# Layer 0: output projection of seven token tiles as partial sums in SBUF beside the last pair of heads; compressed keys' sections by token halves

## The chip, the cores and the metric

The kernel runs on one core of a Trainium2 chip. The metric is the device time of one execution in microseconds (us); the kernel before was timed in three runs.

## What is computed

A decoder trunk of two layers over 1024 tokens of width 1024, in float32. Layer 0 mixes with forgetting attention (FoX), layer 1 with native sparse attention (NSA); each adds its projected, gated mixer output to x, and a last RMSNorm follows.

```python
def fox_mixer(h, w_in, b_f, w_out):
    proj = h @ w_in
    q, k, v, f, z = split(proj)                      # 16 heads of 64
    c = cumsum(log_sigmoid(f + b_f))
    logits = q @ k.T * HEAD_DIM ** -0.5 + c[query] - c[key]     # causal
    o = softmax(logits) @ v
    return (o * silu(z)) @ w_out

def reference(x, ...):
    x = x + fox_mixer(rmsnorm(x, norm_g[0]), ...)
    x = x + nsa_mixer(rmsnorm(x, norm_g[1]), ...)
    return rmsnorm(x, final_g)
```

The change concerns the last product of `fox_mixer`, the sum with x behind it, and the first sections of the input projection of `nsa_mixer` (`kc_raw`, the keys to be compressed).

## The kernel before

**Products.** A float32 product is made of two-part operands (a high part rounded by a cast, a low part as the rest). `mm3` (L132) issues three matmuls per 128-row chunk: high by high, high by low, low by high. A projection of one 128-wide section for one half of the tokens (512 columns, one bank of PSUM) is eight chunks, 24 matmuls.

**Layer 0, attention.** Heads go in eight pairs. For each pair `fox_fill` projects k, v, q and z; `FoxDuo` handles two query tiles of 128 (one of each token half) of one head: score matmuls into the three score banks of `ps_s` (L587, L588), a running minimum on VectorE, DVE (L596, into `P`), exp on ScalarE, ACT (L605), the high part as a copy on ACT (L606) and the low part on DVE (L607), a transposing transfer on the DMA queue SP (`pT<-hl`, L608), and two duos later the PV matmuls (L621, L622) into a bank of `ps_a`, with the evictions L633 and L635. When a pair is done, `o` is transposed on PE (`pto`, L643), scaled and gated (L645) and stored to `oF` in DRAM (L646), one row block of 128 per pair and token half.

**What sets the order.** `merge` draws PE work from two generators: `fox_main` (scores and PV, with costs) and `fox_fill`. For each unit of cost of the main work it draws 2.3 units of fill (`PACE`; `LAST`, 2.6, for the last eight duos). A fill that yields a condition is blocked until it holds. On each engine the instructions stand in the order a scheduler gives them, and are executed in that order.

**Layer 0, output projection.** `load_wout` fetches half of the output weights (512 rows) into a tile, and splits them: casts on ACT, low parts (`wo<-wo,wo`, L539) on GpSimd (POOL). `out_start` runs in the fill of the last pair: for token tiles 4, 5 and 6 it loads row blocks of `oF` (`of<-oF`, L482, one staging tile `wst`), splits them (L476 on ACT, L477 on DVE) and multiplies them by the weights into PSUM banks that are kept until the end: chunks 0 to 3 of tiles 4 and 5, later 4 to 6, then 0 to 6 of tile 6, and at the end chunk 7 of all three. `out_layer` does the rest behind the attention: for tile 7 and 0 to 3 it loads all eight row blocks (L701), splits them (L702, L703) and multiplies; for each tile it adds x (`xr`, L710), squares with a sum on ACT (L94), takes the root and its inverse (L101, L102), multiplies by the inverse and the gains (`h_n`, L106), stores x (L725), and transposes h on PE (`pth_n`, L116) into `hT`, high part on ACT (L120), low part on DVE (L121).

**Layer 1, first sections.** `cmp_raw` projects a section of the compressed keys or values for both token halves; the two sections of a kind follow each other (`pn_kc`). Their weights are loaded by `load_w` (cast on DVE, L128; low part on POOL, L129) into two pairs of buffers. Behind them come the gates (`pg`, L993, L994).

## Time and profile before

| what | us |
|---|---|
| median of 3 runs (lowest to highest) | 1500.1 (1499.29 to 1501.46) |
| profiled execution, its own time | 1503.75 |
| its span, first to last instruction | 1502.0 |
| PE busy | 1418.6 (94%) |
| DVE busy | 1069.9 (71%) |
| ACT busy | 806.4 (54%) |
| POOL busy | 572.6 (38%) |

One execution was recorded; its own time lies 3.65 us above the median of the runs. The page gives busy time by engine, the same in 40 slices of 37.6 us with the clock that TensorE was granted, and the groups of instructions. Busy time of PE is modelled to the end of each pipelined matmul, so the distance between starts says what one costs.

### The profile page before, as it was taken

Reading aid. Unit: us, or ns where it says so; the run is one execution under the profiler, and the core shown is the slowest. Engines: PE = TensorE matmul, PEld = TensorE weight load, DVE = VectorE, ACT = ScalarE, POOL = GpSimd, SP = SyncE. Lnnn points to the kernel's source line nnn. Section 1 sums busy time; section 2 is a strip of 40 time slices with the busy share of each in tenths; the row PEclk is TensorE's granted clock in tenths of the full one; section 3 lists DMA queues with packets and bytes.
Section 4 is the critical chain, followed back from the end, with each engine's and each line's share of the span. In section 5 each row is a group of like instructions: output and inputs, shape, how many; then the busy total and the mean of one; then the engine's idle time right before and its main releaser. Section 6 shows DMA issues by size and latency. Waiting matters only on the chain.

```text
span 1502.0 us, 29578 instructions
## 1 busy us (share of the span) xinstructions
PE 1418.6 (94%) x10488; PEld 1176.0 (78%) x10488; DVE 1069.9 (71%) x2764; ACT 806.4 (54%) x2029; POOL 572.6 (38%) x612
## 2 busy tenths in 40 slices
PE   5999999999999877899999998989999999989998
PEld 4888888888788666788888876878888888877886
DVE  6586888787787774555745568778888888877745
ACT  5364646555565752324222465457767676766623
POOL 1232232222232610023324233356767666766500
PEclk9999999999999888999999998999999999999999
DMA  7886777877778864541524667585877796787544
GB/s 245 256 177 140 163 154 160 178 148 169 153 163 157 213 116 144 178 152 57 158 83 135 195 158 192 169 218 130 158 188 154 167 174 151 172 201 161 92 138 153
DMA packets 405875, 242.92 MB, mean 162 GB/s; under 512 B 332576, under 2 KB 353312, under 8 KB 405472
## 3 DMA queue, kind: packets, MB, share of 16 engines
q1 hardware_dynamic: 405728, 241.03, 66.5%
q8 instruction: 83, 1.36, 0.4%
q14 instruction: 64, 0.52, 0.1%
HBM read 121.16 MB, written 44.11 MB: 110 GB/s over the span
## 4 chain that ended last, share of the span: by engine, by line
PE 67%; DVE 16%; ACT 6%; DMA 5%; issue 4%; POOL 2%; SPq 0%; DVEq 0%; ACTq 0%; POOLq 0%
PE S_n L1331 6%; PE y L133 4%; PE y L135 4%; PE y L134 3%; PE ptp_n L1363 3%; PE v L133 2%; PE v L135 2%; PE v L134 2%; PE S L587 2%; PE S L588 2%; PE k L133 2%; PE O L621 2%; PE k L134 2%; DVE hl L607 2%; PE k L135 2%
## 5 line engine op out<-in xcount | busy, mean ns | idle before, releaser
L1341 ACT ACTIVATE P_n<-P_n,m_n 128x640 f32<-128x640 f32 (+7 forms) x256 | 187.4, 733 | 69.1 <-DVE m_n L1340 43.4
L1331 PE MATMUL S_n<-nk,nq 128*128 128x320 f32 (+5 forms) x768 | 178.6, 347 | 10.8 <-DVE m_n L1338 7.5
L605 ACT ACTIVATE P<-P,m 128x512 f32<-128x512 f32 (+1 forms) x192 | 116.9, 610 | 132.0 <-DVE m L596 131.2
L576 POOL TENSOR_TENSOR Bd<-B,tri 128x128 f32<-128x128 f32 x128 | 62.3, 502 | 245.4 <-DVE m L596 227.3
L1345 POOL TENSOR_TENSOR hl_n<-P_n,hl_n 128x640 f16<-128x640 f32 (+4 forms) x128 | 142.9, 1116 | 9.4
L1331 PEld LDWEIGHTS S_n<-nk,nq 128*128 128x128 f32 x768 | 126.0, 192 | 23.5 <-DVE m_n L1338 9.7
L607 DVE SCALAR_TENSOR_TENSOR hl<-P,hl 128x512 f16<-128x512 f32 (+1 forms) x192 | 124.0, 663 | 19.9 <-ACT hl L606 18.9
L1338 DVE CUSTOM_DVE_ANT_0 P_n<-S_n,wmask 128x640 f32<-128x640 f32 (+2 forms) x192 | 112.9, 595 | 23.7 <-PE S_n L1331 20.0
L1344 POOL CAST hl_n<-P_n 128x640 f16<-128x640 f32 (+4 forms) x128 | 74.8, 584 | 119.5 <-ACT P_n L1341 108.6
L150 ACT ACTIVATE pth_n<-ptp_n 128x512 f16<-128x512 f32 (+1 forms) x160 | 86.6, 546 | 54.9 <-PE ptp_n L1363 53.9
L151 DVE SCALAR_TENSOR_TENSOR ptl_n<-ptp_n,pth_n 128x512 f16<-128x512 f32 (+1 forms) x160 | 100.5, 633 | 17.0 <-ACT pth_n L150 15.4
L133 PE MATMUL y<-wo,ohi 128*128 128x512 f32 x230 | 95.4, 415 | 4.5 <-ACT ohi L702 4.5
L1363 PE MATMUL ptp_n<-ident,P_n 128*128 128x128 f32 x576 | 91.5, 279 | 5.3 <-DVE ptl_n L151 3.4
L606 ACT ACTIVATE hl<-P 128x512 f16<-128x512 f32 (+1 forms) x192 | 92.5, 513 | 4.2 <-DMA pT<-hl 2.8
L135 PE MATMUL y<-wo,olo 128*128 128x512 f32 x230 | 92.6, 404 | 1.0 <-DVE olo L703 1.0
L134 PE MATMUL y<-wo,ohi 128*128 128x512 f32 x230 | 92.8, 404 | 0.0
L1363 PEld LDWEIGHTS ptp_n<-ident,P_n 128*128 128x128 f32 x576 | 66.7, 142 | 18.8 <-DVE ptl_n L151 11.3
L587 PE MATMUL S<-KH,Q 128*128 128x512 f32 (+1 forms) x192 | 68.3, 369 | 10.0 <-DVE m L596 9.8
L1338 DVE CUSTOM_DVE_ANT_0 P_n<-S_n,bias 128x640 f32<-128x640 f32 (+1 forms) x64 | 65.1, 1018 | 9.9 <-PE S_n L1331 9.9
L1371 PE MATMUL O_n<-nv,pth_n 128*128 128x64 f16 x576 | 70.5, 195 | 1.1 <-ACT pth_n L150 0.6
L1372 PE MATMUL O_n<-nv,pth_n 128*128 128x64 f16 x576 | 69.6, 193 | 0.0
L1373 PE MATMUL O_n<-nv,ptl_n 128*128 128x64 f16 x576 | 68.4, 193 | 0.0
(398 smaller groups left out, 4530.3 us busy)
## 6 DMA issues: line engine op xcount, KB each, us to landing
nq<-qD SPq DMA_DIRECT2D x64, 256.0 KB
B<-cD SPq DMA_DIRECT2D x16, 512.0 KB
wo<-wD SPq DMA_DIRECT2D x16, 512.0 KB
nq<-qD SPq DMA_DIRECT2D x64, 128.0 KB
x<-in_x_dram SPq DMA_DIRECT2D x8, 512.0 KB
wst_k<-in_fox_w_dram SPq DMA_DIRECT2D x8, 512.0 KB
wst_v<-in_fox_w_dram SPq DMA_DIRECT2D x8, 512.0 KB
wD<-in_fox_w_out_dram SPq DMA_DIRECT2D x8, 512.0 KB
```

The source lines that it names most:

```text
L133: T.matmul(ps, wh, mh, start=first, stop=False, **kw)
L134: T.matmul(ps, wh, ml, start=False, stop=False, **kw)
L135: T.matmul(ps, wl, mh, start=False, stop=last, **kw)
L151: V.scalar_tensor_tensor(lo[:, 0:n], pt[:, 0:n], scale, h, OP.mult, OP.subtract)
L587: T.matmul(ps[:, 0:n], q, KH[j][:, k0:k0 + n], start=True, stop=False)
L605: A.activation(L[:, 0:n], L[:, 0:n], AF.Exp, bias=init, scale=-1.0, accum_out=self.lr[:, col + c:col + c + 1])
L607: V.scalar_tensor_tensor(lo[:, cs], L[:, 0:n], UP, hi[:, cs], OP.mult, OP.subtract)
L1331: T.matmul(ps[:, b, 0:w], self.q[x][:, qi * P:(qi + 1) * P], k[:, k0 + b * w:k0 + b * w + w], start=(x == 0), stop=(x == 1))
L1338: V.tensor_tensor_reduce(dst, src, mk, 1.0, 3e38, OP.add, OP.min, m)
L1341: A.activation(L, L, AF.Exp, bias=m, scale=-1.0, accum_out=self.l[:, y, qi:qi + 1])
L1345: G.tensor_tensor(hl[:, n:2 * n], L, hl[:, 0:n], OP.subtract)
L1363: T.transpose(pt[:, (x + i) * P:(x + i + 1) * P], L[:, kb * P - k0:(kb + 1) * P - k0], ident)
```

## The change

Four parts:

- `out_start` becomes `out_start0`. It works in eleven parts (token tile, first chunk, end): chunks 0 to 3 of tiles 4 to 7, chunks 4 to 6 of the same tiles, chunks 0 to 6 of tiles 0, 1 and 2. Each half of a part is one product in a bank of `ps_a`, which DVE adds at once to `xr`, a tile in SBUF that starts as x. The load and the split of a part are issued between the two halves of the part before. `out_rest0`, in place of `out_layer`, has only chunk 7 of these seven tiles and all of tile 3, then the norms.
- The tiles `KH` and `KL` move to a pool `sk` of their own that lives to the end of the layer; as the keys of a pair are used up, `xr` takes their places.
- In the last pair the order of the fill becomes q and z of tokens 512 to 1023, the first weights' load, q of 0 to 511, the weights' splits, z of 0 to 511, then `out_start0`. `load_wout` yields for each half chunk, and gives every second low part to DVE. `LAST` is gone; `merge` gets a cap of 4000 on the fill's debt.
- `cmp_raw` takes lists of sections: both sections of the compressed keys are projected for tokens 512 to 1023 first, then both for 0 to 511. The values' sections stay as they are.

```diff
+    sk = tc.alloc_tile_pool(name="sk", bufs=4, side="right")
...
-        KH = [sa.tile([P, S], F32R, tag="KH", bufs=4, name=f"KH_{p}_{j}") for j in range(2)]
+        KH = [sk.tile([P, S], F32R, tag="KH", name=f"KH_{p}_{j}") for j in range(2)]
...
-                for half in (1, 0):
-                    yield from fox_q(p, wq, (half,))
-                    yield from fox_z(p, wz, (half,))
-                    yield from load_wout(hp, 0, half)
-        yield from out_start()
+                yield from fox_q(p, wq, (1,))
+                yield from fox_z(p, wz, (1,))
+                rows0 = load_wout(hp, 0, 1)
+                yield next(rows0)
+                yield from fox_q(p, wq, (0,))
+                yield from rows0
+                yield from fox_z(p, wz, (0,))
+                yield from out_start0(load_wout(hp, 0, 0))
...
+    def out_start0(rows1):
+        yield next(rows1)
+        parts = [(t, 0, 4) for t in (4, 5, 6, 7)] + [(t, 4, 7) for t in (4, 5, 6, 7)] + [(t, 0, 7) for t in (0, 1, 2)]
+        def met(n):
+            t, _, stop = parts[n]
+            return (("o", stop - 1, t // 4) in ready and ("scored", 6) in ready
+                    and (t >= 4 or "scores" in ready))
+        def load(n):
+            t, k, stop = parts[n]
+            if t not in xs0:
+                xs0[t] = sk.tile([P, D], F32, tag=("KH", "KL")[t % 2], name=f"xr0_{t}")
+                dma(xs0[t], a["x"][t * P:(t + 1) * P, :])
+            pend[n] = wp.tile([P, KC, P], F32, tag="wst", bufs=1, name=f"of0_{t}_{k}"), *out_parts(f"0_{t}_{k}")
+            dma(pend[n][0][:, k:stop, :], oF[k * P:stop * P, t * P:(t + 1) * P].rearrange("(k p) t -> p k t", p=P))
...
+        for n, (t, k0, stop) in enumerate(parts):
+            if n == 2:
+                yield from rows1
+            more = n + 1 < len(parts)
+            soon = more and met(n + 1)
+            for half in range(2):
+                if soon:
+                    (load, split)[half](n + 1)
+                _, oh, ol = pend[n]
+                pt = ps_a(f"y0_{t}_{k0}_{half}")
+                cs = slice(half * 512, half * 512 + 512)
+                for k in range(k0, stop):
                     wh, wl = ready["wout"][k // 4]
+                    mm3(pt, oh[:, k, :], ol[:, k, :], wh[:, k % 4, cs], wl[:, k % 4, cs], k == k0, k == stop - 1)
                     yield 650
+                V.tensor_tensor(xs0[t][:, cs], pt, xs0[t][:, cs], OP.add)
+            if more and not soon:
+                yield lambda n=n: met(n + 1)
+                load(n + 1)
+                yield 1000
+                split(n + 1)
...
-        if i:
-            yield 0
+        yield 0
         for k in range(4):
             for c in range(2):
-                if i:
-                    yield 400
+                yield 400 if i else 200
...
-                (V if i and c else G).tensor_tensor(lo[:, k, cs], f(lo[:, k, cs]), f(hi[:, k, cs]), OP.subtract)
-            yield 200
+                (V if c else G).tensor_tensor(lo[:, k, cs], f(lo[:, k, cs]), f(hi[:, k, cs]), OP.subtract)
...
-    merge(fox_main(), fox_fill(), PACE, rebase=True)
+    merge(fox_main(), fox_fill(), PACE, rebase=True, cap=4000)
...
+    def out_rest0(ow, w, after):
...
+        for t in (4, 5, 6, 7, 3, 0, 1, 2):
...
+            for half, cs in enumerate(cols2):
+                pt = (ps_s, ps_a)[t % 2](f"y0_{t}_{half}")
+                if t == 3:
+                    for k in range(7):
+                        wh, wl = w[k // 4]
+                        mm3(pt, oh[:, k, :], ol[:, k, :], wh[:, k % 4, cs], wl[:, k % 4, cs], k == 0, False)
+                wh, wl = w[1]
+                mm3(pt, lh[:, tk], ll[:, tk], wh[:, 3, cs], wl[:, 3, cs], t != 3, True)
+                V.tensor_tensor(xs0[t][:, cs], pt, xs0[t][:, cs], OP.add)
+                nm.square(cs)
+            pend.append((t, xs0[t], nm.finish(gB, 2)))
+            if len(pend) > 2:
+                after(*pend.pop(0))
...
+        for part in parts:
+            yield from section([(kind, i) for i in part], lambda half, pt, n, part=part: use(half, pt, part[n]))
+        ready[kind, "raw"] = True
...
-        for i in range(2):
-            yield from cmp_raw("kc", i)
+        yield from cmp_raw("kc", ((0, 1),))
```

How instructions move is shown at three places (names with a last number that only tells buffers apart).

DVE in the last pair, around the third duo of its first head, whose scores fill `P_0_3` and whose minimum is L596 before and L604 after. Before:

```order
L596 ISA P_0_3_0_1_6479,m_0_3_0_6477<-S_0_3_0_1_6478,Bd_0_3_0_6475,m_0_3_0_6477 128x128
L596 ISA m_0_3_0_6477 128x1
L631 RECIPROCAL l_0_1_6275<-l_0_1_6275 128x2
L630 TENSOR_TENSOR l_0_2_6400<-l_0_2_6400 128x1
L596 ISA P_0_3_0_0_6485,m_0_3_0_6477<-S_0_3_0_0_6484,B_0_6176,m_0_3_0_6477 128x512
L596 ISA m_0_3_0_6477 128x1
L607 SCALAR_TENSOR_TENSOR hl_0_2_6398<-P_0_2_0_1_6418,hl_0_2_6398 128x384
L477 TENSOR_TENSOR olo_6124<-of_4_6341,ohi_6123 128x384
L607 SCALAR_TENSOR_TENSOR hl_0_2_6398<-P_0_2_0_0_6424,hl_0_2_6398 128x512
L633 TENSOR_REDUCE ot_0_1_6517<-O_0_1_6496 128x128
```

The same place after the change:

```order
L604 ISA P_0_3_0_1_6529,m_0_3_0_6527<-S_0_3_0_1_6528,Bd_0_3_0_6525,m_0_3_0_6527 128x128
L604 ISA m_0_3_0_6527 128x1
L615 SCALAR_TENSOR_TENSOR hl_0_3_6510<-P_0_3_1_0_6517,hl_0_3_6510 128x128
L604 ISA P_0_3_0_0_6535,m_0_3_0_6527<-S_0_3_0_0_6534,B_0_6161,m_0_3_0_6527 128x512
L604 ISA m_0_3_0_6527 128x1
L519 TENSOR_TENSOR xr_4_6129<-y_4_4_0_6497,xr_4_6129 128x512
L519 TENSOR_TENSOR xr_4_6129<-y_4_4_1_6552,xr_4_6129 128x512
L638 TENSOR_TENSOR l_0_3_6512<-l_0_3_6512 128x1
L639 RECIPROCAL l_0_3_6512<-l_0_3_6512 128x2
L615 SCALAR_TENSOR_TENSOR hl_0_3_6510<-P_0_3_0_1_6529,hl_0_3_6510 128x512
L615 SCALAR_TENSOR_TENSOR hl_0_3_6510<-P_0_3_0_0_6535,hl_0_3_6510 128x512
L641 TENSOR_REDUCE ot_0_1_6598<-O_0_1_6562 128x128
```

Two additions of product banks (L519) stand between a duo's minimum and its low parts; there are 22 of them in the pair.

ACT at the pair's seventh duo (`P_1_2`, `hl_1_2`). Before:

```order
L605 ACTIVATE P_1_2_1_0_6650,l_1_2_6645<-P_1_2_1_0_6650,m_1_2_1_6648 128x256
L606 ACTIVATE hl_1_2_6643<-P_1_2_1_0_6650 128x256
L605 ACTIVATE P_1_2_0_1_6663,l_1_2_6645<-P_1_2_0_1_6663,m_1_2_0_6661 128x384
L605 ACTIVATE P_1_2_0_0_6669,l_1_2_6645<-P_1_2_0_0_6669,m_1_2_0_6661 128x512
L606 ACTIVATE hl_1_2_6643<-P_1_2_0_1_6663 128x384
L606 ACTIVATE hl_1_2_6643<-P_1_2_0_0_6669 128x512
```

And after the change:

```order
L613 ACTIVATE P_1_2_1_0_6791,l_1_2_6786<-P_1_2_1_0_6791,m_1_2_1_6789 128x256
L497 CAST ohi_1_0_6915<-of_1_0_6914 128x896
L614 ACTIVATE hl_1_2_6784<-P_1_2_1_0_6791 128x256
L613 ACTIVATE P_1_2_0_1_6804,l_1_2_6786<-P_1_2_0_1_6804,m_1_2_0_6802 128x384
L613 ACTIVATE P_1_2_0_0_6810,l_1_2_6786<-P_1_2_0_0_6810,m_1_2_0_6802 128x512
L614 ACTIVATE hl_1_2_6784<-P_1_2_0_1_6804 128x384
L614 ACTIVATE hl_1_2_6784<-P_1_2_0_0_6810 128x512
```

The cast of the loaded chunks of token tile 1 (L497) stands between the first exp of the duo and its copy.

DVE in the output layer after the change, where tile 7's norm ends and tile 3's product comes in; `whi_nkc` is the weight cast for the second section of the compressed keys:

```order
L106 SCALAR_TENSOR_TENSOR h_n_7_7234<-xr_7_6353,st_n_7_7233,gB_7145 128x512 x2
L121 TENSOR_TENSOR hT_1_1_7141<-pth_n_5_1_7260,hT_1_0_7140 128x4x128
L718 TENSOR_TENSOR xr_3_7151<-y_3_0_7271,xr_3_7151 128x512
L128 CAST whi_nkc_7534<-wst_nkc_7532 128x1024
L718 TENSOR_TENSOR xr_3_7151<-y_3_1_7298,xr_3_7151 128x512
L121 TENSOR_TENSOR hT_1_1_7141<-pth_n_6_0_7331,hT_1_0_7140 128x4x128
L100 TENSOR_TENSOR st_n_3_7269<-st_n_3_7269 128x1
```

Before, the same cast stood between the two additions of tile 3 too, but tile 3 was the last of the layer; now tiles 0, 1 and 2 come behind it.

## Rows read from the trace of the kernel before

**Rows 1.** The page: the span in 40 slices, PE's busy tenths and its clock.
```profile
PE   5999999999999877899999998989999999989998
PEclk9999999999999888999999998999999999999999
```

**Rows 2.** Windows: length, PE, PEld, DVE, ACT, POOL busy; clock, DMA share, GB/s.
```profile
405.00:468.00 63.00, 63.00 (x405) 52.04 (x403) 50.90 (x152) 36.54 (x93) 17.48 (x20) 1.00 0.78 165
500.00:591.00 91.00, 72.33 (x439) 56.07 (x437) 57.31 (x183) 43.85 (x112) 25.37 (x29) 0.83 0.59 127
591.00:669.00 78.00, 70.45 (x321) 57.03 (x322) 41.65 (x74) 27.73 (x63) 8.02 (x8) 0.96 0.51 172
...
440.00:450.00 10.00, 10.00 (x61) 8.24 (x60) 9.79 (x29) 4.80 (x12) 4.17 (x5) 1.00 0.68 163
```

**Rows 3.** PE's waits, 500 to 591 (three) and 591 to 669: total, times, longest.
```profile
PE S L587 <- DVE m L596: 9.8, 9, 2.7
PE O L621 <- DMA pT<-hl: 3.1, 2, 1.9
PE O L621 <- DVE ot L633: 2.9, 2, 2.5
...
PE y L133 <- ACT ohi L702: 4.5, 2, 2.3
```

**Rows 4.** Timeline of PE at the marks: start, length, instruction.
```profile
405.08 0.38 PE L643 MATMUL pto<-ident,o 128*128 128x128 f32 x2
...
468.35 0.49 PE L643 MATMUL pto<-ident,o 128*128 128x128 f32 x3
...
507.36 0.63 PE L133 MATMUL y<-wo,ohi 128*128 128x512 f32 x1
...
590.14 0.27 PE L643 MATMUL pto<-ident,o 128*128 128x128 f32 x1
...
668.33 0.40 PE L135 MATMUL pn_kc<-hT,wlo_nkc 128*128 128x512 f32 x1
...
677.22 0.39 PE L135 MATMUL pn_kc<-hT,wlo_nkc 128*128 128x512 f32 x1
...
686.97 0.39 PE L993 MATMUL pg<-hT,gw 128*128 128x512 f32 x1
```

**Rows 5.** PE's groups, one of three alike: 500 to 591 (two), 591 to 669.
```profile
L133 PE MATMUL y<-wo,ohi 128*128 128x512 f32 x32 | 14.6, 457 | 0.0
...
L133 PE MATMUL y<-wo,o_KH 128*128 128x512 f32 x16 | 7.2, 451 | 0.0
...
L133 PE MATMUL y<-wo,ohi 128*128 128x512 f32 x80 | 32.8, 411 | 4.5 <-ACT ohi L702 4.5
...
L116 PE MATMUL pth_n<-ident,h_n 128*128 128x128 f32 x64 | 8.9, 275 | 2.6 <-DVE hT L121 1.4 <-DVE h_n L106 1.2
```

**Rows 6.** DVE's groups, 591 to 669 us: busy, mean ns, idle before and why.
```profile
L106 DVE SCALAR_TENSOR_TENSOR h_n<-xr,st_n,gB 128x512 f32<-128x512 f32 x16 | 11.5, 765 | 0.1
L710 DVE TENSOR_TENSOR xr<-y,xr 128x512 f32<-128x512 f32 x16 | 10.7, 689 | 20.1 <-PE y L135 16.1 <-DMA xr<-in_x_dram 4.0
L121 DVE TENSOR_TENSOR hT<-pth_n,hT 128x512 fp32r<-128x512 f32 x16 | 10.5, 682 | 0.2 <-ACT hT L120 0.2
L703 DVE TENSOR_TENSOR olo<-of,ohi 128x1024 fp32r<-128x1024 f32 x5 | 6.1, 1224 | 5.7 <-ACT ohi L702 5.7
```

**Rows 7.** Timeline of ACT and DVE: a cast behind a load, behind a matmul.
```profile
591.52 1.04 ACT L702 CAST ohi<-of 128x1024 fp32r<-128x1024 f32 x1 [5.26 <-DMA of<-oF]
...
661.91 0.69 DVE L128 CAST whi_nkc<-wst_nkc 128x1024 fp32r<-128x1024 f32 x1 [4.52 <-PE y L134]
```

**Rows 8.** POOL's group, 440 to 700 us; timeline of DVE, two splits.
```profile
L539 POOL TENSOR_TENSOR wo<-wo,wo 128x512 fp32r<-128x512 f32 x16 | 22.2, 1410 | 9.4 <-ACT wo L538 9.4
...
500.86 1.70 DVE L477 TENSOR_TENSOR olo<-of,ohi 128x512 fp32r<-128x512 f32 x1
...
509.76 0.68 DVE L477 TENSOR_TENSOR olo<-of,ohi 128x512 fp32r<-128x512 f32 x1
```

More of the change, by code (lines that the diff above doesn't have):

```diff
@@ new lines, in fox_fill, with split @@
+                yield from fox_z(p, wz, (1,))
[5 more added lines that the diff above has]
+                yield from out_start0(load_wout(hp, 0, 0))
+    xs0 = {}
+    def out_start0(rows1):
+        yield next(rows1)
+        parts = [(t, 0, 4) for t in (4, 5, 6, 7)] + [(t, 4, 7) for t in (4, 5, 6, 7)] + [(t, 0, 7) for t in (0, 1, 2)]
+        pend = {}
+        def met(n):
[9 more added lines that the diff above has]
+            dma(pend[n][0][:, k:stop, :], oF[k * P:stop * P, t * P:(t + 1) * P].rearrange("(k p) t -> p k t", p=P))
+        def split(n):
+            _, k, stop = parts[n]
+            of, oh, ol = (x[:, k:stop, :] for x in pend[n])
+            A.copy(oh, of)
+            V.tensor_tensor(ol, of, f(oh), OP.subtract)
+        yield lambda: met(0)
+        load(0)
+        yield 2000
+        split(0)
+        for n, (t, k0, stop) in enumerate(parts):
[3 more added lines that the diff above has]
+            soon = more and met(n + 1)
+            for half in range(2):
+                if soon:
[4 more added lines that the diff above has]
+                for k in range(k0, stop):
@@ L489, in products @@
                     wh, wl = ready["wout"][k // 4]
-                    cs = slice(half * 512, half * 512 + 512)
-                    mm3(ys[t][half], oh[:, k, :], ol[:, k, :], wh[:, k % 4, cs], wl[:, k % 4, cs], k == 0, k == KC - 1)
+                    mm3(pt, oh[:, k, :], ol[:, k, :], wh[:, k % 4, cs], wl[:, k % 4, cs], k == k0, k == stop - 1)
                     yield 650
-        for t, banks in ((4, (ps_a, ps_s)), (5, (ps_a, ps_t))):
-            ws[t] = out_parts(f"0{t}")
-            ys[t] = [ps(f"y0_{t}_{half}") for half, ps in enumerate(banks)]
-            yield from rows_of(t, slice(0, 4))
-            yield from products(t, slice(0, 4))
@@ L499, in out_start @@
-        for t in (4, 5):
-            yield from rows_of(t, slice(4, 7))
-        ws[6] = [sa.tile([P, S], F32R, tag=x, bufs=4, name=f"o06_{x}").rearrange("p (k t) -> p k t", k=KC) for x in ("KH", "KL")]
-        yield from rows_of(6, slice(0, 7))
-        for t in (4, 5):
-            yield from products(t, slice(4, 7))
-        yield lambda: "scores" in ready
-        ys[6] = [ps_s(f"y0_6_{half}") for half in range(2)]
-        yield from products(6, slice(0, 7))
-        yield lambda: ("o", 7, 1) in ready
@@ L509, in out_start @@
-        for t in (4, 5, 6):
-            split(t, slice(7, 8), ready["z", 7, 1][1][:, (t - 4) * P:(t - 3) * P].rearrange("p (k t) -> p k t", k=1))
-        for t in (4, 5, 6):
-            yield from products(t, slice(7, 8))
+                V.tensor_tensor(xs0[t][:, cs], pt, xs0[t][:, cs], OP.add)
[4 more added lines that the diff above has]
+                split(n + 1)
     def out_parts(name):
@@ L781, in tile_fox_nsa, with cmp_raw, use @@
     raw = {}
-    def cmp_raw(kind, i):
-        if i == 0:
-            raw[kind] = pm.tile([P, GR, S], F32, tag="raw", bufs=1, name=f"raw_{kind}")
-        R = raw[kind]
-        def use(half, pt, n):
+    def cmp_raw(kind, parts):
+        raw[kind] = R = pm.tile([P, GR, S], F32, tag="raw", bufs=1, name=f"raw_{kind}")
+        def use(half, pt, i):
             for j in range(2):
@@ L1150, in nsa_fill @@
         yield lambda: "kcm" in ready
-        for i in range(2):
-            yield from cmp_raw("vc", i)
+        yield from cmp_raw("vc", ((0,), (1,)))
         for i in range(2, 6):
```

76 lines of the change are left out of this document (24 added, 52 removed).

## Prediction

> **What bounds the kernel now.** I read the page's slices first: TensorE (PE) is nearly full everywhere but at the start and in slices 14 to 16, where its digits fall and the granted clock drops to 8 tenths [rows 1]. That is the end of layer 0. The windows sort it by stage [rows 2]. From 405 to 468 us (pair 6: projections beside attention) PE is busy for all 63.00 us at clock 1.00. From 500 to 591 us, the last pair, it is busy for 72.33 of 91 us at clock 0.83. From 591 to 669 us, the output layer, it is 70.45 of 78 us at 0.96. What ended its waits there [rows 3]: in the last pair VectorE (DVE), 9.8 us before score matmuls and 2.9 us before PV matmuls, and the transposed probabilities' transfers, 3.1 us; in the output layer mostly the split of a loaded tile, 4.5 us. So the pair's own chain (scores, minimum, exp, split, transfer, PV) cannot feed PE alone; in pair 6 the projections stand in its gaps, in pair 7 only three lumps of output products do.
>
> **What PE loses there.** A 512-column matmul takes 0.228 us from start to start at full clock: 39 of them lie between 668.33 and 677.22 [rows 4]. Pair 6 lasts 63.27 us between two `pto` groups and holds 192 projection matmuls (43.8 us) and 8 transposes (some 0.9), so a duo of scores and PV costs (63.27 - 44.7) / 8 = 2.32 us of PE. By the same prices:
> - From the first `y` matmul (507.36) to the last `pto` (590.14) are 82.8 us. They hold 144 `y` matmuls [rows 5], 32.8 us, eight duos and two more PVs, some 20.2, and transposes, 1.6: 54.6 us. Lost: 28.2 us; PE idles for 18.7 us in rows 2's window, and the low clock (1.2 in place of 2.4 GHz for a part of the time) makes the rest.
> - From there to the first `pg` (686.97) are 96.8 us. They hold 240 `y` matmuls [rows 5] (54.7), 64 transposes (at 0.115, 7.4) and 96 `pn_kc` matmuls (21.9): 84.0. Lost: 12.8 us.
>
> Together 41.0 us, and some 2 us before the first `y`. That is all that refilling PE can give: the number of matmuls is the same after the change.
>
> **The change part by part.**
> - *Products moved.* 49 of the 64 products of a token tile with a 128-row chunk lie in the fill now, 24 before; each is 6 matmuls. The fill holds 294 `y` matmuls (67.0 us), the output layer 90 (20.5). From the first `y` to the last before row block 7: 67.0 + 20.2 + 1.6 = 88.8 us plus a loss L1. From there to `pg`: 20.5 + 7.4 + 21.9 = 49.8 us plus a loss L2. The sum is 138.6 + L1 + L2 against 179.6 before, so the gain is 41.0 - L1 - L2.
> - *Added to DVE:* 22 additions of a bank into `xr`, 0.69 us each [rows 6] with starts some 0.61 apart (13.4 us); splits of 25 more chunks (0.68 us for four [rows 8], 4 us); eight low parts of the weights taken from POOL (some 0.61 each, 4.9): 22.3 us. With the 57.31 us of before that is 79.6 us in the 96 from 500 to the new end of the fill, 83%; pair 6 has 50.90 of 63, 81%, with PE full. But some 15 of the 22 fall into the pair's first 50 us, on top of 31: about 46 of 50. From 440 to 450 us DVE is busy for 9.79 of 10 us and PE loses nothing [rows 2], so between 0 and 12 I charge 3 us, near that row.
> - *Two duos too close.* Behind the part (7, 4 to 7) the fill is held until the scores are done, so the last two score bursts stand together; there are three score banks, and the longest wait for one was 2.7 us [rows 3]: 2 us (0 to 4).
> - *ACT.* The cast of tile 1's seven chunks stands between an exp and its copy (second excerpt). Such a load held ACT for 5.26 us before [rows 7]. What is late then is the last two PVs' transfers, which already cost PE 1.9 once [rows 3]: 3 us (0 to 5). So **L1 is 8**; its ends, with the rival below, are 3 and 22.
> - *SP.* 11 loads of `oF` and 7 of `x` go in among the transposes of the pair. The DMA share there is 0.59, in pair 6 0.78 with no PE wait [rows 2]: nothing, while the share stays under about 0.8. The row block 7 load, exposed before (the same 5.26 us), now has four groups of 21 matmuls ahead of it, 19 us: hidden; uncovered it would cost those 5 us.
> - *Output layer.* DVE has 16 additions, 16 products with `gB` and 16 low parts as before (10.7, 11.5 and 10.5 us) and three splits of 1.22 fewer [rows 6]: 41.65 - 3.7, some 37 us without the first weights of layer 1. PE has 20.5 + 7.4 and now both first `kc` sections of tokens 512 to 1023 (48 matmuls, 10.9), which need no later tile: 38.8 us. The two are almost even. The weight cast for `kc` waits for a product's last matmul, 4.52 us before [rows 7]; it stands between the two additions of tile 3 (third excerpt), and behind it are some 18 us of DVE work for `hT`. I count 3 us there and 2 for the start of the chain: **L2 is 5** (2 to 12).
> - *Compressed keys by halves:* same matmuls. The weights of `qa` get their buffer 24 matmuls later, with 48 `kc` matmuls and the gates still ahead: nothing; uncovered, one weight split, of some 3 us.
> - *Weights' loading:* 16 POOL operations of 1.41 us become 8 [rows 8]. While POOL ran them, a DVE split of 512 columns took 1.70 us; later one took 0.68. Their removal is a gain before the first `y`: of the 2 us lost there I take 1 back (0 to 2).
> - *Layer 1:* its `load_wout` loses a charge of 200 units behind each of eight chunks, so the last fill runs 1.6 us ahead of its old pace. Nothing, between -2 and 2 us.
>
> Sum: 41.0 - 8 - 5 + 1 = 29 us off the profiled execution's 1503.75. The median of the three runs, 1500.1, stands 3.65 below it, so **1471 us**.
>
> The row on POOL and DVE shows two slow neighbours [rows 8] and no more; by it such an operation is gone for each one added, and the sum is the 1471 above. The second price of the first rival below takes the opposite view.
>
> The Trainium skill, SBUF — State Buffer, section Who interferes with whom, is beside that second price: it says that a VectorE instruction with two SBUF inputs and a GpSimd one that reads SBUF hold a shared port pair exclusively, the second waiting for the whole of the first. By that rule the halves of the weights given to VectorE meet the halves left to GpSimd.
>
> **The rivals.**
> - *VectorE becomes the bound in the last pair.* For it: 46 of 50 us, in order, with waits for ACT inside. Against it: pair 6 with 81%. Priced with 15 of its two-input operations a microsecond longer, as the split at 500.86, and 5 us for the two other places, L1 is 20: gain 17, 1483. The same from another cause: each of the eight subtractions of weights waits for one whole POOL operation, 8 x 1.41 = 11.3 us in the DVE-dense part [rows 8]: 1482. Chance of the two together 0.18.
> - *The output layer runs at the chain of a tile* (DVE's addition, two products and two low parts, 0.69 + 1.5 + 1.4, with ACT's square and root and the transposes some 5.5 us) instead of the pipeline: eight tiles take 44 us where PE has 38.8, and with waits between them L2 is 15: gain about 19, 1481. For it: eight norms in a row on in-order queues. Against it: the order puts steps of three tiles between those of one (third excerpt). Chance 0.08.
> - *Slower: SP's order.* A load of `oF` needs the one staging tile free and stands ahead of transposes; while it waits, so does every transfer behind it, then PV, then the split's buffer. Decides from 41 / 11 = 3.7 us per load on PE: at 4.5 us each, 8 us slower than now, 1508. Against it: the longest wait of PE for a transfer is 1.9 us [rows 3], and two duos lie between a score and its PV. Chance 0.04.
> - *No change:* PE's time is saved but given back in layer 1, whose first weights and tables are loaded behind the stores of `x1`, in a shorter output layer. It would take 26 us or more; they have 11 us of `kc` and the gates ahead. Chance 0.03, 1500.
>
> **How the numbers follow.** The forecast has 0.67: with L1 from 3 to 13 and L2 from 2 to 10, a gain of 19 to 37, 1463 to 1481. At the low end the second microsecond before the first `y` may come back too, and the changed pace of layer 1 give 2: 1460. The first two rivals reach to 1487, with L1 at 22 and L2 at 7 (gain 13). From 1460 to 1487 some 0.85 is held. A measurement here tells 0.2%, 3 us, from nothing: faster 0.93, same 0.03, slower 0.04.
>
> **What would show it.** Right: in the last pair PE near 100% at clock 1.00, DVE near 90%; the fill's end near 603 us (506.4 + 88.8 + 8), the first `pg` near 658. L1 wrong: waits of score matmuls for DVE's minimum of over 8 us, or clock under 0.95 in the pair. L2 wrong: `pth` waits for `h_n` of over 5 us. SP rival: PV waits for `pT` in most duos. The forecast falls if layer 1 after `pg` is over 3 us longer than before, or if PE is full and the fill's end still lies past 615.

## The result, and the profile after

The changed kernel takes 1486.01 us (median of 4 runs, 1483.44 to 1487.03) beside 1500.78 for the kernel before: ratio 0.990, interval 0.9886 to 0.9916. Measured twice more, it has medians of 1484.60 and 1484.98, beside 1501.18 and 1499.71. So it is faster by 15 to 17 us, where 29 were forecast. Single executions of either kernel scatter by several us (the changed one from 1481.7 to 1491.3), so the table takes three profiles of the changed kernel (spans 1481.7, 1483.4, 1489.6) and two of the kernel before (1502.0, 1499.9). The fill, the work drawn in beside the attention, ends at the first product of row block 7 (`y<-wo,o7h`); the kernel before has no such mark.

| us | before | changed, three profiles | mean | forecast |
|---|---|---|---|---|
| first `y` | 507.36, 506.17 | 512.66, 512.45, 513.87 | 513.0 | 506.4 |
| end of the fill | | 611.30, 609.59, 614.00 | 611.6 | 603 |
| first `pg` | 686.97, 686.32 | 666.67, 664.97, 670.22 | 667.3 | 658 |
| from first `pg` to layer 1's first `y` | 660.5, 660.6 | 663.6, 663.2, 666.1 | 664.3 | as before |
| from layer 1's first `y` to the last matmul | 147.5, 146.0 | 144.1, 147.9, 146.0 | 146.0 | as before |

The page of the first profile, the slices of [rows 1]: the hole at slices 14 to 16 is nearly gone, and the clock no longer falls there. The one slice that still shows 8 tenths, the 25th, lies in layer 1 and showed it before.

```profile
PE   5999999999999898999999988989999999989998
...
PEclk9999999999999999999999998999999999999999
```

The windows of [rows 2] in the changed kernel, with one that the prediction did not look at, 484 to 540 us:

```profile
484.00:540.00 56.00, 47.89 (x286) 37.68 (x285) 44.30 (x124) 33.05 (x80) 16.74 (x20) 0.94 0.94 226
500.00:591.00 91.00, 80.88 (x511) 64.63 (x510) 70.78 (x209) 49.63 (x124) 17.20 (x23) 0.94 0.81 186
591.00:669.00 78.00, 74.64 (x354) 61.13 (x353) 50.28 (x93) 29.73 (x69) 14.01 (x13) 0.98 0.43 140
...
513.00:611.00 98.00, 91.48 (x537) 73.99 (x537) 66.82 (x186) 41.78 (x103) 11.49 (x17) 0.95 0.74 175
```

The same new window of the kernel before:

```profile
484.00:540.00 56.00, 46.87 (x291) 36.40 (x289) 43.39 (x128) 35.63 (x87) 30.16 (x32) 0.88 0.82 189
```

From 500 to 591 us PE is busy for 80.88 us where it was 72.33, at clock 0.94 in place of 0.83: the refilling took place. In the fill (513 to 611) DVE is busy for 68%, not near 90. But the share of the DMA engines between 484 and 540 us, 0.82 before, is 0.94. That is a mean too: the engines are full from 484 to 504 and from 512 to 540 (1.01), and at 0.51 in the 8 us between, just ahead of the first `y`, where DVE is busy for 7.87 of 8 us and PE for 4.53:

```profile
504.00:512.00 8.00, 4.53 (x29) 3.03 (x26) 7.87 (x24) 5.96 (x13) 4.34 (x5) 0.98 0.51 108
```

In the kernel before DVE was as full there (7.70 of 8).

PE's waits in the changed kernel, before the first `y` (468 to 513 us, one row), in the fill (513 to 611, three), in the output layer (611 to 667, two):

```profile
PE S L595 <- DVE m L604: 5.7, 4, 2.3
...
PE O L629 <- DMA pT<-hl: 3.5, 2, 3.2
PE y L133 <- ACT ohi L497: 1.7, 1, 1.7
PE S L595 <- DVE m L604: 1.3, 2, 0.9
...
PE pth_n L116 <- DVE h_n L106: 2.0, 1, 2.0
PE pth_n L116 <- DVE hT L121: 1.3, 3, 0.6
```

The same wait for the minimum in the kernel before, from 468 us to the first `y` and from there to 591:

```profile
PE S L587 <- DVE m L596: 2.6, 2, 1.9
...
PE S L587 <- DVE m L596: 7.9, 8, 2.7
```

From the first `y` on it fell from 7.9 to 1.3 us. Ahead of the first `y` it grew from 2.6 to 5.7, and this is now the largest sum, where the prediction expected none. PE stands idle for 6.5 us of the fill in all; the rest of its loss there goes with the clock (0.95). The timelines of SP, then ACT and DVE, show how it comes about (the idle time before a row stands in brackets):

```profile
484.42 1.00 SPq L490 DMA_DIRECT2D xr<-in_x_dram  x2
485.52 0.38 SPq L568 DMA_DIRECT2D B<-cD  x1
485.99 6.13 SPq L616 DMA_TRANSPOSE pT<-hl  x1
492.22 0.53 SPq L542 DMA_DIRECT2D wo<-wD  x1
...
496.37 1.14 ACT L548 CAST wo<-wo 128x512 fp32r<-128x512 f32 x2 [5.31 <-DMA wo<-wD]
...
497.54 1.34 DVE L549 TENSOR_TENSOR wo<-wo,wo 128x512 fp32r<-128x512 f32 x1 [3.90 <-ACT wo L548]
498.80 0.74 DVE L604 CUSTOM_DVE_ANT_0 P<-S,B,m 128x512 f32<-128x512 f32 x1
```

The same place on SP and ACT in the kernel before:

```profile
484.44 0.53 SPq L560 DMA_DIRECT2D B<-cD  x1
485.18 3.90 SPq L608 DMA_TRANSPOSE pT<-hl  x1
489.17 0.53 SPq L530 DMA_DIRECT2D wo<-wD  x1
...
493.56 1.14 ACT L538 CAST wo<-wo 128x512 fp32r<-128x512 f32 x2 [2.47 <-DMA wo<-wD]
```

Two loads of x (1 MB) go out ahead of the first weights. The transpose behind them keeps SP for 6.13 us in place of 3.90, the weight's load is issued 3.05 us later, and its cast starts 2.81 later. DVE, which now has every second low part, stands in line behind that cast for 3.90 us, with a minimum and so PE's next scores behind it.

### The profile page after: what moved, and what is told of

Same layout as the page of the kernel before. It is cut to its first block, busy times and chain, and to the rows that moved or that the text cites. A ratio compares the mean times of both kernels' runs of the same rounds, so it can differ in the third digit from the quotient of the medians.

```text
span 1481.7 us, 29610 instructions
## 1 busy us (share of the span) xinstructions
PE 1405.8 (95%) x10488; PEld 1165.9 (79%) x10488; DVE 1082.8 (73%) x2795; ACT 806.3 (54%) x2030; POOL 560.7 (38%) x604
## 4 chain that ended last, share of the span: by engine, by line
PE 67%; DVE 15%; ACT 7%; DMA 5%; issue 4%; POOL 1%; SPq 1%; DVEq 0%; ACTq 0%; POOLq 0%
PE S_n L1341 6%; PE y L133 3%; PE ptp_n L1373 3%; PE y L134 3%; PE y L135 3%; PE v L133 2%; PE v L135 2%; PE v L134 2%; DVE P_n L1348 2%; PE S L595 2%; PE k L133 2%; PE O_n L1381 2%; PE S L596 2%; PE k L135 2%; PE k L134 2%
## 5 line engine op out<-in xcount | busy, mean ns | idle before, releaser
L615 DVE SCALAR_TENSOR_TENSOR hl<-P,hl 128x512 f16<-128x512 f32 (+1 forms) x192 | 121.8, 653 | 16.3 <-ACT hl L614 15.3
L1348 DVE CUSTOM_DVE_ANT_0 P_n<-S_n,wmask 128x640 f32<-128x640 f32 (+2 forms) x192 | 112.9, 595 | 18.4 <-PE S_n L1341 15.5
L595 PE MATMUL S<-KH,Q 128*128 128x512 f32 (+1 forms) x192 | 64.5, 352 | 7.4 <-DVE m L604 7.3
```

What stands on the lines that cost most here:

```text
L615: V.scalar_tensor_tensor(lo[:, cs], L[:, 0:n], UP, hi[:, cs], OP.mult, OP.subtract)
L1348: V.tensor_tensor_reduce(dst, src, mk, 1.0, 3e38, OP.add, OP.min, m)
```

## The experiments

Medians of all runs, and marks from one profile of each (`pn_qa` is the first product behind the gates; in the kernel before it comes 13.7 us behind `pg`). e5 and e14 leave x, and e6 most of the partial sums, out of the result:

| run | median, ratio to before (interval) | first `y` | fill's end | first `pg` | to `pn_qa` |
|---|---|---|---|---|---|
| c_before | 1500.26, 0.9995 (0.9985 to 1.0006) | 506.17 | | 686.32 | 13.7 |
| c_after | 1484.60, 0.989 (0.9875 to 0.9904) | 512.45 | 609.59 | 664.97 | 14.9 |
| r_after | 1484.98, 0.9901 (0.9885 to 0.9917) | 513.87 | 614.00 | 670.22 | 16.2 |
| e1_lows_pool | 1490.97, 0.9931 (0.9919 to 0.9944) | 511.70 | 617.77 | 673.16 | 14.9 |
| e2_x_behind_w | 1487.69, 0.9902 (0.9885 to 0.9919) | 509.88 | 612.59 | 668.01 | 16.7 |
| e3_both | 1491.97, 0.9941 (0.9928 to 0.9953) | 508.42 | 616.74 | 671.67 | 14.9 |
| e5_no_x_loads | 1480.16, 0.9861 (0.9842 to 0.9881) | 510.08 | 605.88 | 660.36 | 14.8 |
| e6_add_1_column | 1487.43, 0.9907 (0.9892 to 0.9923) | 511.92 | 612.95 | 668.32 | 16.3 |
| e7_loads_earlier | 1483.28, 0.9873 (0.9855 to 0.9890) | 513.69 | 606.04 | 661.42 | 16.4 |
| e8_kc_by_section | 1484.14, 0.9879 (0.9862 to 0.9897) | 513.41 | 611.79 | 667.18 | 13.5 |
| e10_x_late | 1487.75, 0.9902 (0.9888 to 0.9916) | 507.93 | 606.94 | 668.63 | 16.3 |
| e11_lows_vector_alone | 1501.11, 1.0003 (0.9992 to 1.0015) | 508.71 | | 683.25 | 13.6 |
| e12_x_twice | 1488.68, 0.9909 (0.9892 to 0.9926) | 514.01 | 614.35 | 669.33 | 14.9 |
| e13_early_and_section | 1476.35, 0.9832 (0.9815 to 0.9849) | 514.70 | 609.41 | 664.78 | 13.6 |
| r_e13_early_and_section | 1477.69, 0.985 (0.9836 to 0.9863) | 512.22 | 606.71 | 662.09 | 13.6 |
| e14_early_no_x | 1478.89, 0.9844 (0.9828 to 0.9860) | 509.17 | 602.58 | 658.75 | 16.3 |
| e15_layer1_pace | 1485.75, 0.9892 (0.9877 to 0.9907) | 513.65 | 611.71 | 666.96 | 14.8 |

**Both kernels once more.** No edit.

> The changed kernel once more, unchanged, with a second profile: the first one came from the fastest of its four runs (1483.44 against a median of 1486.01), the profile of before from the slowest of its own (1503.72 against 1500.78), so the two profiled spans lie 20.3 us apart and the medians 14.8. Theory A (the gain is 20, the runs scatter): ratio 0.986 to 0.988. Rival (the gain is 15, the profiled pair was a lucky one): ratio 0.990, and the second profile's span lies 2 to 4 us above 1481.7, with the longer part somewhere that can be named.

> The kernel before once more, with a second profile. Theory A (what lies behind the first pg scatters by some 3 us whatever the kernel, and the first profile of before came from a slow execution): the stretch up to the first pg is within 1 us of 686.97, and the stretch behind it differs from the 815.0 of the first profile by up to 4 us either way. Rival (the two profiled executions differ in layer 0): first pg off by more than 1.5 us.

The second profile of the changed kernel has the same marks within 1.7 us, and its ratio, 0.989, lies between the two that were expected. The gain up to `pg` stands again; behind `pg` the changed kernel is some 3 us longer (the table at the top). The profile that the prediction rests on came from an execution above its median, but layer 0 lies within 1.2 us of the second one.

**The line on DVE, and the late weights.** e1:

```diff
-                (V if c else G).tensor_tensor(lo[:, k, cs], f(lo[:, k, cs]), f(hi[:, k, cs]), OP.subtract)
+                (V if i and c else G).tensor_tensor(lo[:, k, cs], f(lo[:, k, cs]), f(hi[:, k, cs]), OP.subtract)
```

> The changed kernel with all sixteen low parts of layer 0's output weights on POOL again, as before the change. Theory A (VectorE stands in line): in the changed kernel VectorE idles for 3.90 us up to 497.54 at such a low part, whose weight has not landed, with the next minimum behind it, and PE loses 2.4 us there and 3.6 while VectorE catches up; without it the first y product comes 3 to 5 us earlier than at 512.66 and the time falls by 3 to 5 us. Theory B (the weights' load is late, whoever splits it: ACT's cast stands before an exp for 5.3 us): the first y product moves by less than 1.5 us, the time by less than 2. Theory C (POOL's sixteen operations slow VectorE, as in the kernel before): first y not earlier, the time up by 1 to 4 us.

e2 (e3 is both):

```diff
         for k in range(4):
...
+        ready.setdefault("wo_in", f(lo[:, 3, 0:1]))
         yield 0
...
                 xs0[t] = sk.tile([P, D], F32, tag=("KH", "KL")[t % 2], name=f"xr0_{t}")
+                if t in (4, 5):
+                    G.tensor_copy(xs0[t][:, 0:1], ready["wo_in"])
                 dma(xs0[t], a["x"][t * P:(t + 1) * P, :])
```

> The changed kernel with the loads of x for token tiles 4 and 5 (1 MB) put behind the load of the first weights, by a one-column copy that reads a weight before x is loaded over it. Theory B: the first weight lands some 2.8 us earlier (its cast at 493.6 in place of 496.37), VectorE idles for about 1 us in place of 3.9, the first y product comes 2.5 to 4 us earlier and the time falls by 2 to 4 us. Theory A alone: VectorE still stands in line, but for the time that the load still takes; the same sign, less than 2 us. If SP was not what held the weights: the cast stays within 1 us of 496.4 and nothing moves.

> Both edits together. If A and B are one chain (late load, then line on VectorE), the gains do not add: first y at 507 to 508.5, as in the kernel before (507.36), and 4 to 5 us off the time of the changed kernel. If they are two separate losses, 6 to 8 us.

Theory B has its marks. In e2 the first weight is cast at 493.63 and DVE stands for 2.03 us (timelines of ACT and DVE):

```profile
493.63 1.14 ACT L551 CAST wo<-wo 128x512 fp32r<-128x512 f32 x2 [3.44 <-DMA wo<-wD]
...
494.80 1.37 DVE L552 TENSOR_TENSOR wo<-wo,wo 128x512 fp32r<-128x512 f32 x1 [2.03 <-ACT wo L551]
```

The first `y` comes 3.1 us earlier, with both edits 4.6. But no time is won: the fill ends at 612.59 (e2) and 616.74 (e3), and the interval of e2 overlaps the changed kernel's. What is gained ahead of the first `y` is lost again in the fill, so an earlier first `y` does not by itself bring time, and theory A, by which the line on DVE costs 3 to 5 us, falls: all low parts on POOL are 6 us slower, which none of the three theories forecast. ACT's waits in e1, 484 to 600 us:

```profile
ACT ohi L497 <- DMA of<-oF: 13.6, 6, 4.5
ACT wo L548 <- DMA wo<-wD: 13.1, 5, 5.7
```

and in the changed kernel:

```profile
ACT ohi L497 <- DMA of<-oF: 13.3, 5, 5.6
...
ACT wo L548 <- DMA wo<-wD: 7.0, 2, 5.3
```

With the low parts on POOL two of the four loads of the second half of the weights also moved behind two transposes on SP, and ACT waited nearly twice as long for weights. Theory C, POOL slowing DVE, is seen in two groups of DVE from 484 to 600 us, the splits of 512 columns (976 ns in place of 686, four of them) and the low parts of 256 (636 in place of 417, six): some 2.5 us of work. Which of these costs the 6 us was not separated. In both kernels ACT, which has every exp, waits for 20 us or more at casts whose load has not landed.

**The amount of data, and the amount of DVE work.** e5 leaves x out of the sums of tiles 4 to 7, e12 loads it twice, e6 leaves out all but two columns of the 22 partial sums:

```diff
-                dma(xs0[t], a["x"][t * P:(t + 1) * P, :])
+                if t < 4:
+                    dma(xs0[t], a["x"][t * P:(t + 1) * P, :])
...
-                V.tensor_tensor(xs0[t][:, cs], pt, xs0[t][:, cs], OP.add)
+                if t >= 4 and k0 == 0:
+                    V.tensor_copy(xs0[t][:, cs], pt)
+                else:
+                    V.tensor_tensor(xs0[t][:, cs], pt, xs0[t][:, cs], OP.add)
```

> The changed kernel without the loads of x for token tiles 4 to 7 (2 MB; their sums start from the product, so x is left out of these tokens), the same number of VectorE operations. Theory D (the transfers are the bound from 484 to 540 us: share of the DMA engines 0.94 there in the changed kernel, 0.82 before; every load that is moved delays another, so that putting x behind the weights gained 2.6 us before the first y and lost them again): less is moved, so the first y comes 2 to 4 us earlier, ACT waits for loads for less than 12 us in place of 20.8, and the time falls by 5 to 9 us. Theory E (VectorE's amount of work is the bound): less than 2 us. Rival to both (the places in the in-order queues): between, 2 to 5, with ACT's waits only shifted.

```diff
-                dma(xs0[t], a["x"][t * P:(t + 1) * P, :])
+                for _ in range(2 if t >= 4 else 1):
+                    dma(xs0[t], a["x"][t * P:(t + 1) * P, :])
```

> The changed kernel with x for tiles 4 to 7 loaded twice over (2 MB more, same data). Theory D: the reverse of the run without these loads (4.4 us faster for 2 MB less): 4 to 8 us slower, first y 2 to 4 us later, ACT's waits for loads above 24 us. Rival (only the two loads that stand ahead of the first weights count, and the queue has room behind them): the first y later by up to 3 us, the time up by less than 2.

```diff
-                V.tensor_tensor(xs0[t][:, cs], pt, xs0[t][:, cs], OP.add)
+                c1 = slice(half * 512, half * 512 + 1)
+                V.tensor_tensor(xs0[t][:, c1], pt[:, 0:1], xs0[t][:, c1], OP.add)
```

> The changed kernel with the 22 additions of the last pair on one column of each bank in place of 512 (the partial sums are left out but for two columns), so that each waits and releases as before but takes some 0.1 us: VectorE has about 13 us less to do between 512 and 612 us. Theory E (VectorE is the bound in the pair): PE loses 6 to 10 us less in the fill, the time falls by as much. Theory D: less than 3 us.

The window 484 to 540 us of e5, then of e12:

```profile
484.00:540.00 56.00, 50.31 (x307) 39.82 (x306) 47.71 (x133) 33.59 (x83) 18.10 (x22) 0.97 0.84 195
```

```profile
484.00:540.00 56.00, 45.72 (x266) 35.84 (x265) 43.83 (x122) 33.09 (x80) 17.84 (x22) 0.88 1.00 245
```

With the DMA share at 0.84, 0.94 and 1.00, PE is busy for 50.31, 47.89 and 45.72 us there, the fill ends at 605.9, 611.6 and 614.4, and the medians are 1480.2, about 1485 and 1488.7. Taking 2 MB away wins 4 to 6 us, about 2 per MB (the interval of e5 lies below two of the three of the changed kernel and overlaps the third); adding 2 MB costs PE some 2 us in this window, but in the time the loss of 3 to 4 us is not clear of the scatter, for the interval of e12 overlaps all three of the changed kernel.

So theory D has its sign but not its measure. ACT's waits for loads, `of<-oF` and `wo<-wD` together, are 18.4 us in e5, where less than 12 were expected, and 18.3 in e12, where more than 24 were, beside 20.3 in the changed kernel. And the DMA engines are not full in the 8 us ahead of the first `y`. The rival "between", the places in the in-order queues, describes it as well, and the two are not separated: e5 takes away the data and the places of its loads on SP at once.

Theory E falls for the fill. The window 512 to 560 us, the changed kernel (c_after), then e6:

```profile
512.00:560.00 48.00, 45.82 (x283) 37.14 (x282) 39.60 (x113) 26.22 (x68) 10.37 (x15) 0.99 0.88 208
```

```profile
512.00:560.00 48.00, 45.26 (x268) 36.61 (x267) 34.32 (x109) 25.87 (x67) 10.74 (x15) 0.95 0.87 195
```

DVE is freed of 5.3 us in these 48, and of 8 to 9 in the whole fill, and nothing is gained. e6 says nothing on the 8 us ahead of the first `y`, where DVE is full and has none of the 22 additions yet.

**Loads further ahead.** e7, cut to its core (a second staging tile of four chunks, in the pool `sa`; the first eight parts alternate between the two):

```diff
+            if n % 2 and n < 8:
+                pend[n] = sa.tile([P, 4, P], F32, tag="of0", bufs=1, name=f"of0_{t}_{k}")[:, 0:stop - k, :],
...
-                if soon:
-                    (load, split)[half](n + 1)
+                if soon and half == 0:
+                    while at < len(parts) and at <= (n + 2 if n < 6 else n + 1) and met(at):
+                        load(at)
+                        at += 1
+                if soon and half == 1:
+                    split(n + 1)
```

> The changed kernel with a second staging tile, so that the eight loads of oF for tiles 4 to 7 are issued two parts ahead in place of one. Theory F (ACT stands in line at casts whose load has not landed: it waits 13.7 us for of<-oF, in five places): that wait falls under 6 us, the y wait for ohi (1.35) goes, and the time falls by 2 to 5 us. Theory D: the loads are longer under way, not earlier landed; ACT's wait falls by less than a third and the time by less than 1.5 us.

> The changed kernel with loads of oF two parts ahead and without x for tiles 4 to 7 (left out of the sums). If the amount of data between 484 and 540 us and ACT's place in line behind a load are two separate losses, the gains add: fill's end at 600 to 602 (610.5 in the changed kernel, 606 with either edit), the time 8 us below it. If they are one (whatever lets the loads land before ACT needs them): fill's end at 604 to 606, 3 to 5 us below.

PE's waits in the fill of e7, 514 to 606 us, and one of ACT's, 484 to 600:

```profile
PE O L639 <- DMA pT<-hl: 2.8, 3, 2.0
PE y L133 <- DVE xr L528: 1.7, 1, 1.7
PE S L605 <- DVE m L614: 0.3, 1, 0.3
...
ACT ohi L501 <- DMA of<-oF: 12.0, 3, 8.5
```

The wait of `y` for `ohi` and nearly all waits of scores are gone, and the fill ends 5.6 us earlier than in the mean of the changed kernel (4.2 in the mean of the three profiles with these loads: e7, and e13 twice below). The time of e7 alone is not clear of the changed kernel's. ACT's wait for `of<-oF` fell only to 12.0 us, in three places in place of five; 8.5 of it is one wait. So theory F is right on PE, not on its own measure; on that measure it is theory D's sign that came. In e14 the fill ends 9.0 us earlier than in the changed kernel, where the two edits alone gave 5.6 and 5.7: for the most part two losses. The median gains no more than about 6 of it; of the rest, 16.3 us from `pg` to `pn_qa` show some (the next experiment says what they are).

**The keys' sections.**

```diff
-        yield from cmp_raw("kc", ((0, 1),))
+        yield from cmp_raw("kc", ((0,), (1,)))
```

> The changed kernel with the two sections of the compressed keys one after the other again, as before the change. The sum held 10.9 us of PE work for this in the output layer (48 matmuls that need no later tile in place of 24), at no cost behind. If that holds, the part between the fill's end and the first pg is 2 to 5 us longer and the time goes up by as much. If the output layer is set by the chain of a tile: 5 to 8 us. If the order of these sections does not matter: within 1 us.

From the fill's end to `pg` are 55.4 us in e8 and 55.4 in the first profile of the changed kernel: the order buys nothing there. Behind `pg` the halves cost 1.2 us at least. PE's timeline at the first product of the keys' perceptron, the changed kernel, then e8:

```profile
671.49 0.38 PE L133 MATMUL hid_kc<-bh_kc,w1h_kc 128*128 128x252 f32 x1 [1.26 <-ACT bh_kc L838]
...
681.40 0.39 PE L133 MATMUL pn_qa<-hT,whi_nqa 128*128 128x512 f32 x1
```

```profile
670.81 0.38 PE L133 MATMUL hid_kc<-bh_kc,w1h_kc 128*128 128x252 f32 x1
...
680.72 0.39 PE L133 MATMUL pn_qa<-hT,whi_nqa 128*128 128x512 f32 x1
```

With halves, both sections of tokens 0 to 511, which come last, are finished together, and PE waits 1.26 us for ACT's first operand from them; section by section it does not wait. From `pg` to `pn_qa` the six profiles with one section after the other (both of the kernel before and e11 among them) take 13.5 to 13.7 us. The thirteen with halves fall into two groups: seven take 14.7 to 14.9 and six 16.2 to 16.7. What tells these apart is the clock: 1.00 in the seven, 0.89 to 0.90 in the six. The first profile of the changed kernel, then the third (r_after):

```profile
666.67:681.40 14.73, 12.70 (x71) 10.19 (x70) 9.06 (x16) 8.68 (x13) 5.83 (x5) 1.00 0.28 86
```

```profile
670.22:686.40 16.18, 14.12 (x72) 11.52 (x70) 9.59 (x16) 8.74 (x13) 5.30 (x5) 0.89 0.24 81
```

In r_after some matmuls of the gates start 0.43 us apart in place of 0.23, at the lower of the clock's two levels (1.2 and 2.4 GHz). PE's wait ahead of them is the same in both (1.26 and 1.29 us); why the clock fell in one and not in the other stays open. The 16.3 us of e14 are of the slower group (0.90).

**Smaller ones.** e10 loads x for tiles 4 to 7 in thirds of a bank behind the first sums and adds it on POOL (24 operations), with e7's loads.

> The changed kernel with two of the edits that helped, without leaving anything out: the second staging tile (loads of oF two parts ahead), and the first sums of tiles 4 to 7 copied in place of added, so that x for these tokens is not loaded between 484 and 540 us but in thirds of a bank behind 550 us and added by POOL. If the DMA engines between 484 and 540 are what costs: first y at 510, fill's end 602 to 605, time 4 to 9 us below the changed kernel. Rival (POOL's 24 additions slow VectorE or hold up tile 4's norm): the fill's end as before or later, within 2 us of the changed kernel or slower.

The first `y` came at 507.93, earlier than expected, and the fill ended at 606.94, 2 us behind the expected 602 to 605 and no earlier than with e7's loads alone. The output layer then lost what was won, 61.7 us in place of 55.4; PE's waits, 607 to 668 us:

```profile
PE pth_n L116 <- DVE hT L121: 4.2, 3, 2.9
PE pth_n L116 <- DVE h_n L106: 2.5, 1, 2.5
```

DVE waits there for POOL's additions (3.1 us), and the clock is 0.92, where the changed kernel has 0.97. So the rival is right on the time and on a norm held up, not on the fill's end. e11 gives every second low part to DVE in the kernel before (the `i and` taken away there):

> The kernel before with one part of the change alone: every second low part of layer 0's weights on VectorE. The prediction gave this 1 us of gain before the first y (0 to 2). Theory of the line on VectorE: the first y 1 to 2 us later than 507.36 and no gain. From the run with all sixteen on POOL, which made the changed kernel 6 us slower: up to 4 us of gain, from the second half of the weights being ready earlier.

The first `y` comes 1.4 to 2.5 us later, `pg` some 3 earlier, and the time is the same: no gain by itself. e15 restores the old charge (`if i: yield 200` behind each chunk's parts):

> The changed kernel with layer 1's output weights charged as before the change (200 units behind each chunk). The prediction counted nothing for it, between -2 and 2. The changed kernels need 663 to 664 us from the first pg to layer 1's first y product where the kernels before need 660.6: if the changed charge is behind it, 660.6 again and 2 to 3 us off the time; if it is what layer 1 starts with (the order of the keys' sections, the state of the loads), 663 to 664 again, within 1.5 us.

It takes 662.3 us from `pg` to layer 1's first `y`, and the median is the changed kernel's. The stretch itself tells little: in runs whose edits lie in layer 0 it goes from 660.9 (e6) to 666.1 us (e2). So the charge is not seen in the time, and an effect of 1 or 2 us in that stretch is not excluded.

**A version that beats both.** e7's loads with e8's sections, run twice, the second time beside the changed kernel:

> The changed kernel with loads of oF two parts ahead and the compressed keys' sections one after the other again: the two edits that leave nothing out and looked no worse. In their own runs the first pg came at 661.4 (4 to 5 us earlier than in the changed kernel) and the stretch from pg to the first pn_qa took 13.5 us in place of 14.8 (16.4 with the early loads). If both hold together: first pg at 661 to 662, 13.5 behind it, a time 4 to 7 us below the changed kernel. If the early loads only shift the wait into layer 1 whatever the order of sections (16.4 again): within 2 us.

> The changed kernel beside the version with both edits, on one chip. If the 8 us between their medians (1484.6 and 1476.35, in different calls) are real, they stand again, with intervals that don't touch: 0.989 to 0.990 here.

> The version with loads of oF two parts ahead and the keys' sections one after the other, once more: its five executions ran from 1474.2 to 1483.7, and the profiled one was the slowest. If the gain over the changed kernel is real: ratio 0.983 to 0.985, and a second profile has its first pg at 660 to 662, the slow one having lost 3 us in the fill. If the median was luck: ratio 0.987 to 0.988, as with the early loads alone.

1476.35 and 1477.69 us: 22 to 25 us below the kernel before, and 7 below the changed one on the same chip, with intervals that do not touch. The first profile has its `pg` at 664.78, later than the expected 661 to 662, the second at 662.09; both have 13.6 us behind it. So the two edits hold together: some 4 us in the fill, and 1 to 2.5 behind `pg`. The page's slices of it:

```profile
PE   5999999999999899999999988989999999989998
...
PEclk9999999999999999999999999999999999999999
```

## Why the prediction was right or wrong

The direction and the main mechanism held: PE's idle time and low clock at the end of layer 0 were the price to win, and refilling won about half of the 29 us. The measured time lies behind the forecast's own 1463 to 1481; that it lies within 1460 to 1487 is luck, for that end of the range was held for the first two rivals, which are not what happened.

The step that failed is the bullet *SP*, by which the loads cost "nothing, while the share stays under about 0.8". The fill ended at 611.6 where 603 was forecast. With x's loads for four tiles left out and the loads of `oF` further ahead (e14, one profile) it ends at 602.58. So what was put at nothing is, at this mark, as large as the whole miss of 8.4 us. By the steps of the prediction, with the means of the first table:

- **Before the first `y`.** *Weights' loading* took 1 us back; measured are 5.6 us lost (513.0 against 507.36). Miss: 6.6 us, half of the whole. For the bullet *SP* the prediction read a mean of 0.59 over 500 to 591 us; the loads go in from 484 on, where the share was 0.82 before and is 0.94 now. And the order on SP has the two loads of x ahead of the first weights. That low parts on DVE put its queue behind a load was not counted either: alone in the kernel before (e11) they make the first `y` 1.4 to 2.5 us later, not 1 earlier. Both edits together (e3) give 4.6 of the 6.6 back at this mark; the rest stays open. But the marks are not causes: e2 and e3 won here and lost it again in the fill.
- **L1**, 8 us: 611.6 - 513.0 - 88.8 = 9.8. Size right by some luck, parts not: in the first profile the transfer of the last PVs but one took 3.2 (3 forecast), the last score bursts 1.3 (2); DVE's density, priced at 3, is not seen in the fill, though before the first `y` it is; 1.7 are a split behind its load, which the bullet *SP* had at nothing; and some 3 go with the clock at 0.95.
- **L2**, 5 us: 667.3 - 611.6 - 49.8 = 5.9. Right in size, with `h_n` at 2.0 and `hT` at 1.3 as the largest waits. But the 48 `kc` matmuls that "need no later tile" gave nothing there (e8).
- **Layer 1 and the keys by halves**, nothing: 3.1 us longer (3.8 up to layer 1's first `y`, 0.7 given back behind it). That is just past the 3 us by which the prediction said it would fall. The halves are 1.1 to 1.2 of it in two profiles and 2.5 in the third, where the clock falls behind them; the rest, some 1.5 us, stays open, and the changed charge was not separated from it.

The misses, 6.6 + 1.8 + 0.9 + 3.1 = 12.4, leave 16.6 of the 29 us; the medians say 15 to 17.

The first rival stands near the measured time, 1483, but not by its price: e6 took the additions away and gained nothing, and DVE was busy for 68% of the fill. What it named, DVE in order with waits for ACT inside, did occur ahead of the first `y` (5.7 us of PE's waits), but e1, which took that line away, was slower. Nor did its second price come. The eight low parts of weights on DVE, 484 to 612 us, and POOL's eight, 440 to 700, in the changed kernel:

```profile
L549 DVE TENSOR_TENSOR wo<-wo,wo 128x512 fp32r<-128x512 f32 x8 | 6.6, 830 | 3.9 <-ACT wo L548 3.9
```

```profile
L549 POOL TENSOR_TENSOR wo<-wo,wo 128x512 fp32r<-128x512 f32 x8 | 10.4, 1309 | 19.1 <-ACT wo L548 15.4 <-PE S L596 3.7
```

At 0.68 us each the eight would take 5.4; they took 6.6. Three of them overlap an operation of POOL in the timelines, and these three took 1.34, 1.00 and 0.90 us; the other five took 0.67 to 0.69. By the Trainium skill, SBUF — State Buffer, section Who interferes with whom, two such operations that meet share an exclusive lock, and the later one waits until the earlier is done; the trace agrees, but as they rarely met the price is 1.2 us in all, and not 11.3.

The rival on SP's order named the right queue and the wrong victim: PV waits for transposes in two places of the fill only (3.5 us); it was the weights, and the loads of `oF` that ACT splits, that came late.

## What to carry to other kernels

Read the share of the DMA engines in the very stretch into which new loads go, not in a window around it, and read on the queue what they stand ahead of: 1 MB ahead of a weight cost 3 us here, and putting it behind the weight only moved the loss. Where an in-order engine splits what is loaded, try the load two steps ahead (here the fill ended some 4 us earlier): a wait of that engine holds up everything behind it, and a low part given to a faster engine puts that engine in the same line. A gain in one stage is to be followed past the mark where it was won: the order of two sections, thought free, gave nothing before the mark and cost 1.2 us or more behind it. And a first product that comes earlier is no gain by itself, if what it was waiting for is only moved.

## What was not expected of the hardware

A DMA transpose kept SP for 6.13 us behind two loads of x and one of B, 512 KB each, for 3.90 behind B alone, and the same transpose for 3.59 in e2, behind B alone (timeline of SP):

```profile
484.29 3.59 SPq L619 DMA_TRANSPOSE pT<-hl  x1
```

It stands in other profiles too: 6.1 to 6.5 us behind the loads of x in c_after, r_after, e1, e7 and e12, 3.8 without them in c_before and e5. So here the bulk loads delayed not only what they moved ahead of, but also lengthened the time that the queue took for the next transpose. And single executions of one kernel differ by as much as most of these edits are worth: three profiles of the changed kernel have their first `pg` between 664.97 and 670.22 us.
